# Attention units' exponentials, divisions, roundings and rests first on their engines, and head norms' scaling freed from the next tile's sums

## The chip, the cores and the metric

The kernel runs on one core of a Trainium2 chip. The metric is device time in microseconds (us) from the start to the end of one execution; less is better. TensorE (PE) multiplies matrices, VectorE (DVE) and ScalarE (ACT) do elementwise work, GpSimd (POOL) does small elementwise work and issues accumulating loads, SyncE (SP) issues most loads.

## The reference

One layer of a hybrid decoder trunk over 16 meta tokens and 512 real tokens, model width 1024, all in float32:

```python
h = h + 0.5 * swiglu(rms_norm(h, ffn1_norm), ffn1_w_in, ffn1_w_out)      # D_FF = 2816
h = h + token_mixer(rms_norm(h, mix_norm), ...)
h = h + 0.5 * swiglu(rms_norm(h, ffn2_norm), ffn2_w_in, ffn2_w_out)
return h[:, 128:]                                                        # real tokens only

def token_mixer(h, ...):
    qa, ka, va, fa, qb, kb, vb, ga, gb = split(h @ w_in)
    qa, ka, qb, kb = rms_norm of each head (64 wide), with a gain
    log_f = log_sigmoid(fa + forget_bias)
    o_fox = softmax(qa ka^T / 8 + cumsum(log_f)_q - cumsum(log_f)_k, causal) va        # 8 heads
    o_swa = softmax over a window of 128 keys, 16 meta keys and a sink, with a bias by distance   # 8 query, 2 key heads
    return (sigmoid(ga) * (o_fox @ w_branch_fox) + sigmoid(gb) * (o_swa @ w_branch_swa)) @ w_out
```

## The kernel before

Each float32 operand of a matmul is carried as two parts: a rounded part (`hi`, L130, a cast on ScalarE) and the rest (`lo`, L136, a subtraction on VectorE). A product is then three matmuls, L301, L302 and L304 in `prod`: rounded by rounded, rounded by rest, rest by rounded. Weights arrive by DMA as raw pieces and are split the same way in `split_to` (tiles wh and wl), up to three pieces ahead of their use. Most of the FFNs' products, and the gates', take seven half-size products instead of eight, with sums of inputs formed on VectorE (tc, S).

The program has three stages. The first FFN takes about the first 370 us, the token mixer and its output the next 370, the second FFN the rest. In the mixer two kinds of work are woven step by step into one stream (`weave`, `main` and `fills`, from L1628):

- attention units: eight `fox_pair` units (two query blocks of two heads each) and eight `swa_unit` units (one query block of four heads). A unit has `scores` (matmuls at L1292 for fox pairs, `prod` for sliding units; then VectorE adds the bias and takes the row minimum, L1310 or L1460; then `normalise`: exponentials on ScalarE with their sums, a reciprocal and a multiplication by it on VectorE, the "division"), `turn` (TensorE transposes, L1350 or L1473; a rounding into pH, a rest into pL or, for the meta keys, into other rows of pH), and `values` (matmuls at L1359 to L1365 or L1488 and L1490, then `both_halves` moves the result out of PSUM with ScalarE, L1105, and VectorE, L1106). A unit's `turn` and `values` stand behind the next unit's `scores`.
- fills: projections of queries, keys and values in chunks of up to five token tiles (`tok_chunk`), gates and branch products. A query or key tile goes through `head_norm`: squares on ScalarE (L1057), sums and a scaled shift on VectorE (L1058, L1059, the instruction kept in `shared["ts"]`), an inverse root on GpSimd (`rsq`, L351), and later the scaling (`scale`, L1073) on VectorE, which reads the projection out of PSUM and writes qn. `tok_chunk` traces the scaling of tile i - 1 behind the sums of tile i; the last tile's comes in the chunk's `end`. When all tiles are scaled, `finish` transposes qn (L1153, L1161, L1407) into the chunk's queries or keys.

Every engine runs its instructions in one fixed order, which a planner writes down ahead of the run: it goes through the program with a model of the time and, when an engine is free, takes among the instructions that are ready the one traced first. `tc.high_priority()` around instructions lets them be taken ahead of those traced before. `tc.issue_after(i)` and the kernel's `after(...)` place what is traced inside them, on the engine of instruction i, behind i in that engine's order; they wait for nothing else. PSUM tiles come in two groups of four banks, ps and pt, which the planner hands out again when the last reader is done.

In the mixer's end (L1646 to L1700) three gates go through sigmoids on ScalarE, held behind the last exponential by `after(shared["exp"])`, and are multiplied into the branch results on VectorE (L1654). Then the buffers of the mixer are given up, and the buffers of the gates' stage take their place, among them `spare` (L1695) and `xg`.

Of the kernel before, what the change touches and what calls it, by code (L numbers as in the profile page):

```python
# [13 lines left out]
AF = mybir.ActivationFunctionType  # L14
ALU = mybir.AluOpType
# [67 lines left out]
def kernel(  # L83
# [22 lines left out]
    V, A, G, PE, SP = nc.vector, nc.scalar, nc.gpsimd, nc.tensor, nc.sync  # L106
# [23 lines left out]
    def hi(o, i, scale=None):  # L130

        if scale is None:
            return A.copy(o, i)  # L133
        return A.activation(o, i, AF.Identity, scale=scale)

    def lo(o, i, h, scale=None):  # L136

        h = h.bitcast(F32)
        if scale is None:
            return V.tensor_tensor(out=o, in0=i, in1=h, op=ALU.subtract)  # L140
        else:
            return V.scalar_tensor_tensor(out=o, in0=i, scalar=scale, in1=h, op0=ALU.mult, op1=ALU.subtract)  # L142
# [59 lines left out]
    shared = {}  # L202
# [61 lines left out]
    def split_to(n):  # L264
        while state["split"] < min(n, len(pieces)):
            c = state["split"]
            load_to(c + 1)
            state["split"] += 1
            raw = raws.pop(c)
            if callable(raw):  # L270
                with tc.issue_after(shared["lo"]):
                    raw = raw()
            raw, nk, w = raw
            if pieces[c][0] == "D":
                wd = shared["wd"]()
                wh, wl = wd[:, :512], wd[:, 512:1024]
            else:
                wh, wl = (wp.tile([P, PW], F32R, tag=t, name=nm(t)) for t in ("wh", "wl"))
            b = slice(0, nk * w)
            shared["split"] = hi(wh[:, b], raw[:, b]), lo(wl[:, b], raw[:, b], wh[:, b])  # L280
            shared["lo"] = getattr(shared["split"][1], "ins", shared["split"][1])
            split[c] = tuple(t[:, : nk * w].rearrange("p (k c) -> p k c", c=w) for t in (wh, wl))

# [768 lines left out]
    def head_norm(ps, i, nh, outs):  # L1052

        n = M if i == 0 else P
        sq = new("hsq", [P, 256], F32, 3)
        ss = mp.tile([P, 4], F32, tag="hss", name=nm("hss"), bufs=4)[:n, :nh]
        A.activation(sq[:n, : nh * HD], ps[:n, : nh * HD], AF.Square)  # L1057
        V.tensor_reduce(out=ss, in_=sq[:n, : nh * HD].rearrange("p (h d) -> p h d", d=HD), axis=AX.X, op=ALU.add)  # L1058
        ts = V.tensor_scalar(ss, ss, r1sq[:n, i : i + 1], EPS, op0=ALU.mult, op1=ALU.add)  # L1059
        shared["ts"] = getattr(ts, "ins", ts)  # L1060
        rsq(ss, ss)
        src, by = ps[:n, : nh * HD].rearrange("p (h d) -> p h d", d=HD), bc(ss, 2, HD)

        def scale():

            with tc.issue_after(shared["ts"]):
                r = r1[:n, i : i + 1]
                for o in outs:
                    a, b = src, by
                    if isinstance(o, tuple):  # L1070
                        o, par = o
                        a, b = (v.rearrange("p (a b) d -> p a b d", b=2)[:, :, par] for v in (src, by))
                    V.scalar_tensor_tensor(out=o, in0=a, scalar=r, in1=b, op0=ALU.mult, op1=ALU.mult)  # L1073

        return scale
# [4 lines left out]
    def meta_rest(p, ps, w):  # L1080

        lo(p[REST : REST + M, :w], ps[:M, :w], p[:M, :w])
# [122 lines left out]
    def normalise(parts):  # L1205

        l = new("l", [P, 4], F32, 2)[:, : len(parts)]
        for j, (t, nmx) in enumerate(parts):
            shared["exp"] = A.activation(t, t, AF.Exp, bias=nmx, scale=-1.0, accum_out=l[:, j : j + 1])  # L1209
        V.reciprocal(l, l)  # L1210
        for j, (t, _) in enumerate(parts):
            V.tensor_scalar(t, t, l[:, j : j + 1], None, op0=ALU.mult)


    cbs = {}
# [33 lines left out]
    def fox_pair(box, p, ip, before):  # L1249
# [82 lines left out]
        def turn(hh):  # L1332
            if hh == 0:
                ps, pM = psum(), new("pH", [P, 512], bufs=3)
                for b in range(2):
                    c = column(0, 0, b)
                    PE.transpose(ps[:, P * b : P * b + P], ts_[b][:, c : c + P], ident)
                w = slice(0, 2 * P)
                hi(pM[:, w], ps[:, w])
                lo(pM[2 * REST :, w], ps[: 2 * REST, w], pM[: 2 * REST, w])  # L1340
                pts[0] = pM
            for j0 in range(1, nt, 2):
                ps = psum()
                pH, pL = new("pH", [P, 512], bufs=3), new("pL", [P, 512], bufs=3)
                c = 0
                for j in (j0, j0 + 1):
                    pts[j] = pH, pL, c - (P if j == nt - 1 else 0)
                    for b in range(1 if j == nt - 1 else 0, 2):
                        k0 = column(hh, j, b)
                        PE.transpose(ps[:, c : c + P], ts_[b][:, k0 : k0 + P], ident)  # L1350
                        c += P
                hi(pH[:, :c], ps[:, :c])
                lo(pL[:, :c], ps[:, :c], pH[:, :c])

        def values(hh):
            v = box["v"]
# [74 lines left out]
    def swa_unit(box, qbox, g, i, before):  # L1431
        nk = KS if i == 0 else KS + P
        k0 = 0 if i == 0 else KS * (i - 1)
        w = max(nk + nk % 2, 256)
        ts_, pts = [], []
        o = oA[:, 1, 2 * g : 2 * g + 2]

        tiles = [(0, 0), (1, M + 1)] if i == 0 else [(i, 0), (0, P), (i + 1, KS)]

        def scores():  # L1440
            before()
            q, k, b1 = qbox["q"], box["k"], b1s[g]
            room = new("t", [P, 1092], F32)
            for hp in range(2):
                t2 = room[:, 546 * hp : 546 * hp + 546]
                for hh in (2 * hp, 2 * hp + 1):
                    h = 4 * g + hh
                    hb = slice(64 * (hh % 2), 64 * (hh % 2) + 64)
                    ps = psum()
                    sq = (hb, hp, slice(P * i, P * i + P))  # L1450
                    sk = (hb, g, slice(k0, k0 + w))
                    prod([(ps[:, :w], k[0][sk], k[1][sk])], q[0][sq], q[1][sq], True, True)
                    t = t2[:, 273 * (hh % 2) : 273 * (hh % 2) + nk]
                    nmx = new("nmx", [P, 2], F32, 8)
                    init = 3.0e38
                    bias = (
                        [(M + 1, 0, P, b1[:, hh, KS:]), (0, P, KS, bm0[:, h])] if i == 0 else [(0, 0, nk, b1[:, hh])]
                    )
                    for pi, (to, a, b, bt) in enumerate(bias):
                        V.tensor_tensor_reduce(  # L1460
                            out=t[:, to : to + b - a], in0=ps[:, a:b], in1=bt, scale=-0.125, scalar=init,
                            op0=ALU.add, op1=ALU.min, accum_out=nmx[:, pi : pi + 1],
                        )
                        init = nmx[:, pi : pi + 1]
                    ts_.append((t, init))
            normalise(ts_)
            ts_[:] = [t for t, _ in ts_]

        def turn():
            for tt, c0 in tiles:  # L1470
                ps = psum()
                for hh in range(4):
                    PE.transpose(ps[:, P * hh : P * hh + P], ts_[hh][:, c0 : c0 + P], ident)  # L1473
                pH, pL = new("pH", [P, 512], bufs=3), None
                hi(pH, ps)
                if tt:
                    pL = new("pL", [P, 512], bufs=3)
                    lo(pL, ps, pH)
                else:
                    meta_rest(pH, ps, 512)  # L1480
                pts.append((pH, pL))

        def values():
            v = box["v"]
            pv = psum()
            for j, ((tt, c0), (pH, pL)) in enumerate(zip(tiles, pts)):
                st = v[:, tt, P * g : P * g + P]
                PE.matmul(pv, st, pH, start=j == 0, stop=False)  # L1488
                if tt:
                    PE.matmul(pv, st, pL, start=False, stop=j == len(tiles) - 1)  # L1490
            pvv = pv.rearrange("p (a b q) -> p a b q", b=2, q=P)
            for par in range(2):
                hb = slice(64 * par, 64 * par + 64)
                both_halves(o[hb, :, P * i : P * i + P], hb, pvv[:, :, par])

        return [scores, turn, values]
# [219 lines left out]

    def swa_out(m):
        return oA[:, m // 4, m % 4]

    def sliding(*ms):  # L1720
        for m in ms:
# [301 lines left out]
```

## Time and profile before

| | us |
|---|---|
| median of three runs (lowest, highest) | 1076.38 (1075.28, 1077.02) |
| the profiled execution, its own time | 1075.56 |
| its span, first to last instruction | 1073.5 |
| TensorE matmuls busy, share of the span | 1063.2 (99%) |
| VectorE busy | 892.0 (83%) |
| ScalarE busy | 654.6 (61%) |
| GpSimd busy | 211.7 (20%) |

Matmuls overlap in the array and their ends are modelled, so TensorE's busy share hides small holes; the waits of its weight loads (PEld) show them better. In a timeline row the columns are the start in us, the length in us, engine, line, operation, the tile written and those read, the shape and the count; a bracket gives the engine's idle time before it in us and what ended it. "issue" there means that the profile names no release. The granted clock of TensorE was 0.999.

### The profile page before, as it was taken

The page shows a single profiled execution, that of the slowest core. Times are in us where ns is not written, and L with a number is a line of the kernel's source. Part 1 is how long each engine was busy: PE and PEld are TensorE (multiplying, and loading weights), DVE is VectorE, ACT ScalarE, POOL GpSimd, SP SyncE. Part 2 cuts the span into 40 slices and gives each one's busy share as a digit, 9 for nine tenths or more (in the row PEclk, how much of TensorE's full clock was granted, in tenths as well). Part 3 has the DMA queues.
Part 4 walks back from the last instruction along what each step waited for, and adds up shares of the span by engine and source line. Part 5 has one row for each costly group of instructions (what it writes and reads, how often), then busy time and mean ns, then how long its engine had stood idle before and what let it go on. Part 6 is the DMA issues. An engine that isn't in the chain of part 4 may idle for free.

```text
span 1073.5 us, 22262 instructions
## 1 busy us (share of the span) xinstructions
PE 1063.2 (99%) x8515; PEld 1031.0 (96%) x8515; DVE 892.0 (83%) x1725; ACT 654.6 (61%) x1235; POOL 211.7 (20%) x281
## 2 busy tenths in 40 slices
PE   9999999999999999999999999999999999999998
PEld 8999999999999999999878799999999999999998
DVE  7988878888889678789897799888989788877895
ACT  7667456656666455556667766555665466745664
POOL 3011111121124442232200110001122111221120
PEclk9999999999999999999999999999999999999999
DMA  8787777688776314212211874567689777887763
GB/s 279 203 217 164 187 193 198 151 216 219 175 182 178 123 61 126 75 60 73 89 60 42 241 183 125 184 207 195 170 198 194 179 190 170 187 192 196 158 125 101
DMA packets 112570, 173.57 MB, mean 162 GB/s; under 512 B 10880, under 2 KB 59264, under 8 KB 112208
## 3 DMA queue, kind: packets, MB, share of 16 engines
q1 hardware_dynamic: 74464, 122.72, 36.2%
q0 software_dynamic: 29040, 37.83, 22.6%
q10 hardware_dynamic: 8960, 11.60, 3.4%
q8 instruction: 66, 1.08, 0.4%
q14 instruction: 40, 0.33, 0.1%
HBM read 167.89 MB, written 6.32 MB: 162 GB/s over the span
## 4 chain that ended last, share of the span: by engine, by line
PE 47%; DVE 5%; ACT 2%; DMA 1%; issue 1%; POOL 0%; ACTq 0%; SPq 0%; DVEq 0%; POOLq 0%
PE ps L301 8%; PE ps L304 8%; PE ps L302 8%; PE pt L301 7%; PE pt L302 7%; PE pt L304 7%; DVE wl L140 1%; DMA raw<-in_wg_dram 1%; ACT t L1209 1%; ACT wh L133 1%; DVE pL L140 1%; PE ps L1473 0%; PE ps L1938 0%; DVE S L140 0%; PE pt L1473 0%
## 5 line engine op out<-in xcount | busy, mean ns | idle before, releaser
L301 PE MATMUL ps<-x,wh 128*128 128x256 f32 (+2 forms) x768 | 219.7, 286 | 0.1
L302 PE MATMUL ps<-x,wh 128*128 128x256 f32 (+2 forms) x768 | 218.9, 285 | 0.5 <-DVE x L142 0.4
L304 PE MATMUL ps<-x,wl 128*128 128x256 f32 (+2 forms) x768 | 218.9, 285 | 0.0
L140 DVE TENSOR_TENSOR wl<-raw,wh 128x1024 fp32r<-128x1024 f32 (+3 forms) x125 | 150.1, 1201 | 39.8 <-ACT wh L133 38.9
L133 ACT CAST wh<-raw 128x1024 fp32r<-128x1024 f32 (+3 forms) x125 | 128.4, 1029 | 87.7 <-PE ps L302 52.5
L301 PEld LDWEIGHTS ps<-x,wh 128*128 128x128 f32 x768 | 144.7, 189 | 1.7 <-ACT hT L686 0.3
L302 PEld LDWEIGHTS ps<-x,wh 128*128 128x128 f32 x768 | 144.5, 188 | 1.4 <-DVE x L142 0.9
L304 PEld LDWEIGHTS ps<-x,wl 128*128 128x128 f32 x768 | 144.6, 188 | 0.9
L301 PE MATMUL pt<-x,wh 128*128 128x256 f32 (+2 forms) x424 | 125.3, 296 | 0.5 <-ACT wh L133 0.5
L304 PE MATMUL pt<-x,wl 128*128 128x256 f32 (+2 forms) x424 | 124.6, 294 | 0.0
L302 PE MATMUL pt<-x,wh 128*128 128x256 f32 (+2 forms) x392 | 112.5, 287 | 0.0
L133 ACT CAST wh<-tc 128x1024 fp32r<-128x1024 f32 (+1 forms) x70 | 71.8, 1026 | 65.1 <-DVE tc L234 55.7
L140 DVE TENSOR_TENSOR wl<-tc,wh 128x1024 fp32r<-128x1024 f32 (+1 forms) x70 | 83.5, 1192 | 32.4 <-ACT wh L133 32.0
L301 PE MATMUL ps<-acts,wh 128*128 128x264 f32 (+1 forms) x352 | 100.5, 285 | 0.1
L304 PE MATMUL ps<-acts,wl 128*128 128x264 f32 (+1 forms) x352 | 99.8, 284 | 0.0
L302 PE MATMUL ps<-acts,wh 128*128 128x264 f32 (+1 forms) x352 | 99.6, 283 | 0.0
L140 DVE TENSOR_TENSOR wl<-rawC,wh 128x1024 fp32r<-128x1024 f32 (+1 forms) x70 | 84.1, 1201 | 5.9 <-ACT wh L133 5.5
L133 ACT CAST wh<-rawC 128x1024 fp32r<-128x1024 f32 (+1 forms) x70 | 71.6, 1023 | 22.7 <-PE pt L302 17.7
L301 PEld LDWEIGHTS pt<-x,wh 128*128 128x128 f32 x424 | 79.9, 189 | 2.8 <-ACT wh L133 0.7
L304 PEld LDWEIGHTS pt<-x,wl 128*128 128x128 f32 x424 | 79.7, 188 | 2.1
L302 PEld LDWEIGHTS pt<-x,wh 128*128 128x128 f32 x392 | 73.8, 188 | 0.6
L301 PEld LDWEIGHTS ps<-acts,wh 128*128 128x128 f32 x352 | 66.5, 189 | 0.7 <-DVE h2T L918 0.3
(445 smaller groups left out, 3238.8 us busy)
## 6 DMA issues: line engine op xcount, KB each, us to landing
rawC<-in_w1i_dram SPq DMA_DIRECT2D x20, 512.0 KB, 5.1
raw<-in_w1i_dram SPq DMA_DIRECT2D x40, 256.0 KB, 4.5
raw<-in_w2i_dram SPq DMA_DIRECT2D x40, 256.0 KB, 3.3
rawC<-in_w2i_dram SPq DMA_DIRECT2D x20, 512.0 KB, 4.3
raw<-in_wm_dram SPq DMA_DIRECT2D x18, 512.0 KB, 4.3
raw<-in_wout_dram SPq DMA_DIRECT2D x16, 512.0 KB, 4.3
rawD<-in_w1i_dram SPq DMA_DIRECT2D x20, 256.0 KB, 4.3
raw<-in_w1i_dram POOLq DMA_DIRECT2D x20, 256.0 KB, 4.9
```

The source lines that it names most:

```text
L133: return A.copy(o, i)
L140: return V.tensor_tensor(out=o, in0=i, in1=h, op=ALU.subtract)
L301: PE.matmul(ps, sH, mH, start=first, stop=False, **more)
L302: PE.matmul(ps, sH, mL, start=False, stop=False, **more)
L304: shared["mm"] = PE.matmul(ps, sL, mH, start=False, stop=last, **more)
L1209: shared["exp"] = A.activation(t, t, AF.Exp, bias=nmx, scale=-1.0, accum_out=l[:, j : j + 1])
```

## The change

Five edits, all in the mixer:

- `normalise`: exponentials, reciprocal and divisions get high priority.
- `turn` of `fox_pair` and of `swa_unit`: the rounding and the rest of the transposed tile get high priority, and the rest is remembered in `shared["rests"]`. The rest of the very first tile of a fox unit (the meta keys, traced in `turn(0)`) is left as it was, and so are the meta keys' rests of the sliding units in the remembering.
- `split_to`: the rest of a weight piece is placed behind the unit rest remembered last, on VectorE.
- `head_norm`: the scaling is no longer placed behind the sums traced last.
- Before the sliding branch's products, the remembered rest is dropped.

```diff
@@ split_to
-            shared["split"] = hi(wh[:, b], raw[:, b]), lo(wl[:, b], raw[:, b], wh[:, b])
+            with after(*shared.get("rests", ())):
+                shared["split"] = hi(wh[:, b], raw[:, b]), lo(wl[:, b], raw[:, b], wh[:, b])
@@ head_norm
         def scale():
-            with tc.issue_after(shared["ts"]):
+            with ExitStack():
                 r = r1[:n, i : i + 1]
...
@@ normalise
-        for j, (t, nmx) in enumerate(parts):
-            shared["exp"] = A.activation(t, t, AF.Exp, bias=nmx, scale=-1.0, accum_out=l[:, j : j + 1])
-        V.reciprocal(l, l)
-        for j, (t, _) in enumerate(parts):
-            V.tensor_scalar(t, t, l[:, j : j + 1], None, op0=ALU.mult)
+        with tc.high_priority():
+            for j, (t, nmx) in enumerate(parts):
+                shared["exp"] = A.activation(t, t, AF.Exp, bias=nmx, scale=-1.0, accum_out=l[:, j : j + 1])
+            V.reciprocal(l, l)
+            for j, (t, _) in enumerate(parts):
+                V.tensor_scalar(t, t, l[:, j : j + 1], None, op0=ALU.mult)
@@ fox_pair, turn
-                hi(pH[:, :c], ps[:, :c])
-                lo(pL[:, :c], ps[:, :c], pH[:, :c])
+                with tc.high_priority():
+                    hi(pH[:, :c], ps[:, :c])
+                    shared["rests"] = [lo(pL[:, :c], ps[:, :c], pH[:, :c])]
@@ swa_unit, turn
-                hi(pH, ps)
                 if tt:
                     pL = new("pL", [P, 512], bufs=3)
-                    lo(pL, ps, pH)
-                else:
-                    meta_rest(pH, ps, 512)
+                with tc.high_priority():
+                    hi(pH, ps)
+                    if tt:
+                        shared["rests"] = [lo(pL, ps, pH)]
+                    else:
+                        meta_rest(pH, ps, 512)
@@ ahead of sliding
+    shared.pop("rests", None)
     def sliding(*ms):
```

## The prediction

> **What bounds the kernel now.** I read the page's engine totals first, then the busy time by stretches, then TensorE's waits in the mixer, then the chain of waits at the mixer's end, and last the order of instructions around single waits.
>
> ```profile
> span 1073.5 us, 22262 instructions
> PE 1063.2 (99%) x8515; PEld 1031.0 (96%) x8515; DVE 892.0 (83%) x1725; ACT 654.6 (61%) x1235; POOL 211.7 (20%) x281
> ```
>
> ```profile
> 440.00:600.00 160.00, 157.55 (x1114) 137.60 (x1114) 135.28 (x396) 103.65 (x257) 26.48 (x51) 1.00 0.23 72
> 700.00:800.00 100.00, 99.97 (x837) 99.17 (x836) 89.77 (x144) 61.36 (x101) 14.48 (x16) 1.00 0.70 188
> 470.00:490.00 20.00, 19.27 (x165) 17.94 (x162) 18.36 (x66) 13.13 (x37) 5.91 (x15) 1.00 0.16 41
> ```
>
> TensorE bounds the program: in the second FFN its matmuls fill 99.97 of 100 us and its weight loads 99.17. Nothing there is touched by the change, and nothing there can be won. The attention units lie between about 410 and 595 us. There TensorE's weight loads have holes, and VectorE (DVE) has 18.36 of 20 us of work at its densest. So the question is how much TensorE waits in that stretch, and for whom. The stretches' columns are the length, the busy time of TensorE (PE), of its weight loads, of VectorE, ScalarE and GpSimd, the granted clock and the DMA share. The first rows below are the weight-load queue's waits from 382 to 600 us (total, times, longest), the last one is a wait of the matmuls.
>
> ```profile
> PEld pt L1365 <- DVE pL L140: 2.2, 5, 0.7
> PEld pt L1488 <- ACT pH L133: 0.9, 1, 0.9
> PEld pt L1490 <- DVE pL L140: 0.8, 2, 0.6
> PEld pt L1350 <- DVE t L1212: 0.6, 2, 0.3
> PEld ps L1153 <- DVE qn L1073: 0.5, 2, 0.3
> ```
>
> ```profile
> PE ps L1473 <- DVE t L1212: 0.3, 1, 0.3
> ```
>
> That is the whole prize: waits for rests (pL), for roundings (pH), for divided tiles (t) and for head norms' scaling (qn). Added up it is under 6 us, 0.5% of the program, so no reading of this change gives more. The bound of what this kernel can tell from no change is about 0.2%, 2.15 us.
>
> **The rests (lo of pL) first on VectorE: 1.7 us won.** The five waits of L1365 are these rows of the weight-load queue, the wait in brackets.
>
> ```profile
> 463.38 0.19 PEld L1365 LDWEIGHTS pt<-pL,v 128*128 128x128 f32 x1 [0.23 <-DVE pL L140]
> 477.43 0.19 PEld L1365 LDWEIGHTS pt<-pL,v 128*128 128x128 f32 x1 [0.54 <-DVE pL L140]
> 489.61 0.19 PEld L1365 LDWEIGHTS pt<-pL,v 128*128 128x128 f32 x1 [0.31 <-DVE pL L140]
> 513.37 0.19 PEld L1365 LDWEIGHTS pt<-pL,v 128*128 128x128 f32 x1 [0.71 <-DVE pL L140]
> 525.35 0.19 PEld L1365 LDWEIGHTS pt<-pL,v 128*128 128x128 f32 x1 [0.37 <-DVE pL L140]
> ```
>
> They are of two kinds. Here is VectorE ahead of the wait at 489.61, and ScalarE's (ACT) rounding that its rest needs.
>
> ```profile
> 487.38 0.59 ACT L133 CAST pH<-ps 128x512 fp32r<-128x512 f32 x1
> 487.98 0.33 DVE L142 SCALAR_TENSOR_TENSOR v<-ps,r,v 128x128 fp32r<-128x128 f32 x1
> 488.36 0.59 DVE L1073 SCALAR_TENSOR_TENSOR qn<-ps,r,hss 128x128 f32<-128x128 f32 x2
> 488.88 0.67 DVE L140 TENSOR_TENSOR pL<-ps,pH 128x512 fp32r<-128x512 f32 x1
> ```
>
> The rounding was done at 487.97, the rest began at 488.88: a value's rest and two scalings stood in front, all ready earlier in the program's order. A higher priority moves the rest past them by 0.9 us, more than the 0.31 lost. At 477.43 and 525.35 the same kind of instructions stand in front, so I count these three whole: 0.54 + 0.31 + 0.37 = 1.22. The other kind is 513.37:
>
> ```profile
> 510.17 1.04 ACT L133 CAST wh<-raw 128x1024 fp32r<-128x1024 f32 x1
> 511.24 0.59 ACT L133 CAST pH<-pt 128x512 fp32r<-128x512 f32 x1
> 511.51 1.20 DVE L140 TENSOR_TENSOR wl<-raw,wh 128x1024 fp32r<-128x1024 f32 x1
> 512.64 0.67 DVE L140 TENSOR_TENSOR pL<-pt,pH 128x512 fp32r<-128x512 f32 x1
> ```
>
> A weight piece's rounding (1.04) and rest (1.20) went first while the unit's own source was not there yet. Priority alone does not help, since it cannot pass what has begun. The edit in the weight split does help: it queues the split's rest behind the unit rest traced last, which here takes 1.1 us out of the way. But it binds only if the split is traced after the turn, and it leaves ScalarE's cast in front. I count these two waits half, (0.23 + 0.71) / 2 = 0.47. Together 1.7, with ends 0 and 2.2.
>
> What that delays: a weight's rest waits for up to three unit rests of 0.67. Weights are split three pieces ahead of use, so I cost it at nothing; if that cover were gone, each late rest would cost up to 1.2, and the raw buffer's next load on SP's queue would start that much later (the DMA share is 0.23 in this stretch, so a transfer is not pressed). Below nothing it cannot be. No DMA is moved by the change.
>
> **Head norms' scaling freed: 1.2 us won, 0.6 lost.** VectorE and GpSimd (POOL) around a wait of scores for a bank:
>
> ```profile
> 431.55 1.98 POOL L351 TENSOR_TENSOR hss<-hss,nhalf 16x4 f32<-16x4 f32 x2
> 432.58 0.47 DVE L1073 SCALAR_TENSOR_TENSOR qn<-hsq,r,hss 16x256 f32<-16x256 f32 x1 [0.49 <-POOL hss L351]
> 434.78 0.42 DVE L1058 TENSOR_REDUCE hss<-hsq 128x4 f32<-128x256 f32 x1 [0.69 <-ACT hsq L1057]
> 435.24 0.23 DVE L1059 TENSOR_SCALAR hss<-hss,r1sq 128x4 f32<-128x4 f32 x1
> 435.38 0.60 DVE L1073 SCALAR_TENSOR_TENSOR qn<-ps,r,hss 128x128 f32<-128x128 f32 x2
> ```
>
> ```profile
> 436.10 0.18 PEld L1292 LDWEIGHTS ps<-kH,qH 64*128 64x128 f32 x1 [0.73 <-issue]
> 480.34 0.20 PEld L1350 LDWEIGHTS pt<-ident,t 128*128 128x128 f32 x2 [0.43 <-issue]
> ```
>
> The inverse roots ended at 433.53, yet the scaling, which frees the projection's PSUM bank, stood until the next tile's sums at 435.24 were through; VectorE idled 0.69 in between. Scores then waited 0.73. Freed, the scaling can run at about 434.1, behind the two rests there. A second bank wait, 0.43 before transposes, is alike. I take 0.73 + 0.43 = 1.2. The upper end adds the 0.5 of L1153, where a chunk's last scaling feeds the transposes directly.
>
> The loss: nothing now keeps a scaling from being queued directly behind its own sums, where VectorE then stands until GpSimd's inverse root is done. The first row counts the scalings' waits today (us, times), the second tells how long a root takes (min/median/max ns):
>
> ```profile
>   POOL hss L351: 1.8, 3
> ```
>
> ```profile
> L351 POOL TENSOR_TENSOR hss<-hss,nhalf x31: 687/1007/2305, 385.0 to 528.7; 128x4 f32<-128x4 f32 x24, 128x2 f32<-128x2 f32 x4, 16x4 f32<-16x4 f32 x2, 16x2 f32<-16x2 f32 x1
> ```
>
> Of the 31 head norms, the last of each of the seven chunks is free of a later tile's sums of its chunk already; 24 become free. Their price lies between 0 (other work stands between, as before most scalings now) and 0.6 each on VectorE (1.8 / 3). VectorE has 24.7 us of idle time between 440 and 600 (160 - 135.28), so most of this would be absorbed. I take 0.6 us on TensorE in all, one such wait unabsorbed; the ends are 0 and 7.2, which is 24 x 0.6 with half of it absorbed.
>
> **Exponentials and divisions first: 0.3 us won.** ScalarE's exponentials mostly wait for VectorE, not for a turn:
>
> ```profile
> ACT t L1209 <- DVE nmx L1460: 9.4, 7, 2.2
> ```
>
> And VectorE between two heads' divisions:
>
> ```profile
> 416.49 0.47 DVE L142 SCALAR_TENSOR_TENSOR v<-pt,r,v 128x256 fp32r<-128x256 f32 x1
> ```
>
> The scores' subtraction and minimum, which they wait for, gets no priority, so the exponentials themselves win nothing. A division does: the value's rest at 416.49 stands between the first head's division and the second's, and 0.47 of it goes, against one of the two 0.3 waits of L1350. I take 0.3, the ends are 0 and 0.9 (L1350 and L1473). The scores' subtractions get later: up to three unit rests (3 x 0.67) may now pass them. I cost that at nothing because a unit's turn comes only after other units' and projections' matmuls; if that cover is gone it is the 0.3 of L1473 that grows.
>
> **The mixer's end: nothing counted.** L1488 and L1490 wait at 591 to 592 us, 0.9 and 0.8, behind sigmoids. But the chain of waits runs there without TensorE:
>
> ```profile
> 580.64 0.45 PE pt L1473 x4
> 581.13 0.58 ACT pH L133
> ...
> 600.01 7.83 DMA raw<-in_wg_dram
> ...
> 622.02 0.39 PE pt L301
> ```
>
> From 581.13 to 622.02 it is ScalarE, VectorE and one load. A wait removed at 591 returns before 622.02 unless that chain is shorter, and the sigmoids' products (L1654) have to be done before the buffers behind it are free, whatever their order. So nothing, with 1.7 us as the better end. What TensorE wins before 580 does count, since its transposes at 580.64 start this chain.
>
> **The sum.** 1.7 + 1.2 + 0.3 - 0.6 = 2.6 us. The profiled execution took 1075.56 us (span 1073.5 and 2.1 around it); it lies 0.8 below the median of the runs, 1076.38. 1075.56 - 2.6 = 1073.0.
>
> **Rival one: the order hardly changes where TensorE waits (no measurable change).** For it: two of five rest waits have an instruction in front that began before the unit's was ready, VectorE's work stays the same, and at 470 to 490 us it is 92% full, so what moves forward pushes a projection's evacuation back by as much. Against it: 477 to 525 shows ready rests passed over. Then only the scalings' 1.2 is won against 0.6 lost: 1075.0.
>
> **Rival two: VectorE stands for GpSimd (slower).** Place: every freed scaling, in front of whose root nothing else is queued; the high priority cannot pass it, for it is at the queue's head. Without the loss I have 3.2 us won, so the measured slowdown (above 1078.5) needs 6.1 us on TensorE, 0.26 for each of 24 scalings. At half of the 0.6 seen, 7.2 us, the time is 1075.56 - 3.2 + 7.2 = 1079.6. For it: the 0.49 at 432.58 and the mean of 0.6, though scalings are held back now. Against it: VectorE's backlog at 470 to 490 leaves little empty queue, and only three scalings waited at all. A longer root would make it worse:
>
> ```profile
> 511.28 2.31 POOL L351 TENSOR_TENSOR hss<-hss,nhalf 128x4 f32<-128x4 f32 x1 [2.31 <-DVE hss L1059]
> ```
>
> It ran beside the weight's rest of 511.51 and took 2.31, where the median root takes 1.01. The Trainium skill, "SBUF — State Buffer", section "Who interferes with whom", says that a VectorE instruction with two SBUF inputs contends with a GpSimd one that reads SBUF, and that the loser blocks for the whole instruction. By that rule the 1.3 us at 511 is such a block, and a freed scaling behind it would hold VectorE 1.3 longer: the sum would come to 1074.3 with one such meeting and to 1075.6 with two. By the rows, one root in 31 is that long (the median is 1007 ns), and the sum stays.
>
> **Chances.** Forecast 0.46, rival one 0.39, rival two 0.15. Below 1074.2 is faster: 0.46; up to 1078.5 the same: 0.39; slower: 0.15. The better ends of all terms together (2.2 + 1.7 + 0.9 + 1.7, no loss) give 1069.1, all at once unlikely; without the mixer's end it is 1070.8. The range goes from 1070.8 to 1077.6, short of rival two; the forecast's own is 1071.5 to 1074.2.
>
> **What would show it.** Right: L1365's wait for pL falls from 2.2 to about 0.5; no "issue" wait of 0.73 before scores at 436; scalings stand in front of the next tile's sums; weight rests follow unit rests. Wrong: the row of L1073's wait for POOL grows from 1.8 towards 7 and more (rival two); or L1365's wait stays near 2 (rival one); or the waits at 621 to 622 grow by what was won before 580.

## The result, and the profile after

The changed kernel takes 1093.27 us (median of five runs, 1092.71 to 1096.84) against 1076.72 for the kernel before. The ratio of the two kernels' runs, 1.0165 with a 95% interval of 1.0153 to 1.0177, is formed from the single runs and is not the quotient of the two medians (1.0154). By the medians it is 16.5 us slower, and the forecast was 1073.0. The profiled execution, whose rows follow, took 1096.84 us with a span of 1093.7; it is the longest of the five, 3.6 us above their median. The changed kernel's lines lie a few further on: L351 is L352 there, L1073 is L1074, L1365 is L1368, L1695 is L1700.

The page's totals, then busy time by stretches (length, TensorE, weight loads, VectorE, ScalarE, GpSimd, granted clock, DMA share, GB/s):

```profile
span 1093.7 us, 22272 instructions
PE 1069.1 (98%) x8515; PEld 1036.8 (95%) x8515; DVE 894.4 (82%) x1725; ACT 655.0 (60%) x1235; POOL 213.7 (20%) x281
```

```profile
382.00:410.00 28.00, 22.64 (x189) 21.90 (x188) 17.39 (x49) 12.46 (x23) 10.87 (x17) 1.00 0.21 65
410.00:600.00 190.00, 178.13 (x1308) 160.80 (x1309) 148.44 (x443) 106.71 (x271) 36.69 (x73) 0.96 0.22 69
800.00:900.00 100.00, 100.00 (x844) 100.00 (x843) 82.86 (x136) 58.27 (x99) 20.77 (x20) 1.00 0.84 190
```

The same stretch at the start in the kernel before:

```profile
382.00:410.00 28.00, 27.81 (x233) 27.08 (x233) 21.40 (x56) 14.86 (x27) 11.72 (x20) 1.00 0.30 97
```

No work was added: the engines' busy times and counts are those of before within 6 us. In the 28 us from 382 on, 189 matmuls start instead of 233, though no attention unit is at work yet, only projections with their head norms. VectorE is less busy too, 17.39 us for 21.40, so TensorE does not wait for an engine that is full. The second FFN is as full as before. The mixer's end dates the loss: this row is VectorE's first work behind it, first in the kernel before, then in the changed one.

```profile
595.98 2.50 DVE L1695 TENSOR_TENSOR spare<-x 128x512 f32<-128x512 f32 x4
```

```profile
616.10 2.50 DVE L1700 TENSOR_TENSOR spare<-x 128x512 f32<-128x512 f32 x4
```

It comes 20.1 us later, which is the whole difference of the two spans (1093.7 - 1073.5 = 20.2). Now VectorE's waits from 382 to 600 us (total, times, longest), and TensorE's:

```profile
DVE qn L1074 <- POOL hss L352: 27.6, 25, 2.8
DVE hss L1059 <- ACT hsq L1058: 4.1, 6, 1.3
```

```profile
PE ps L303 <- DVE wl L140: 2.9, 1, 2.9
PE pt L1007 <- DVE wl L140: 2.7, 1, 2.7
PE pt L1368 <- DVE pL L140: 2.4, 2, 2.1
PE ps L1368 <- DVE pL L140: 2.0, 2, 1.9
PE ps L1294 <- DVE qn L1074: 1.8, 2, 1.2
PE ps L1294 <- DVE qH L142: 1.3, 1, 1.3
PE ps L1476 <- DVE t L1214: 1.2, 1, 1.2
```

The scalings' wait for the inverse root was 1.8 us in 3 places and is 27.6 in 25. TensorE's seven rows above add up to 14.3 us; the longest such row in the kernel before was this one:

```profile
PE pt L1365 <- DVE pL L140: 1.0, 3, 0.5
```

TensorE now waits for whatever stood behind a scaling in VectorE's queue: weights' rests (wl), unit rests (pL), queries. One such place, VectorE first, then GpSimd, then TensorE:

```profile
455.17 0.23 DVE L1060 TENSOR_SCALAR hss<-hss,r1sq 128x4 f32<-128x4 f32 x1
456.59 0.35 DVE L1074 SCALAR_TENSOR_TENSOR qn<-pt,r,hss 128x128 f32<-128x128 f32 x1 [1.19 <-POOL hss L352]
456.86 0.55 DVE L140 TENSOR_TENSOR pL<-ps,pH 128x384 fp32r<-128x384 f32 x1
```

```profile
455.54 1.01 POOL L352 TENSOR_TENSOR hss<-hss,nhalf 128x4 f32<-128x4 f32 x1 [2.41 <-DVE hss L1060]
```

```profile
457.46 0.39 PE L1368 MATMUL ps<-pL,v 128*128 128x256 f32 x1 [1.87 <-DVE pL L140]
```

The scaling stands directly behind its own shift, VectorE idles 1.19 us for the root, and a unit rest of high priority waits behind it. TensorE loses 1.87. Priority decides who is queued first, not who may pass once VectorE has stopped.

### The profile page after: what moved, and what is told of

The parts are those of the page before. It is cut to its first block, busy times and chain, and to the rows that moved or that the text cites. A ratio compares the mean times of both kernels' runs of the same rounds, so it can differ in the third digit from the quotient of the medians.

```text
span 1093.7 us, 22272 instructions
## 1 busy us (share of the span) xinstructions
PE 1069.1 (98%) x8515; PEld 1036.8 (95%) x8515; DVE 894.4 (82%) x1725; ACT 655.0 (60%) x1235; POOL 213.7 (20%) x281
## 4 chain that ended last, share of the span: by engine, by line
PE 46%; DVE 3%; ACT 2%; DMA 1%; issue 1%; POOL 0%; ACTq 0%; DVEq 0%; POOLq 0%
PE ps L302 8%; PE ps L303 8%; PE ps L305 8%; PE pt L302 7%; PE pt L303 7%; PE pt L305 7%; DMA xg<-h1d 1%; PE ps L1476 1%; DVE wl L140 0%; ACT wh L133 0%; ACT xg L1735 0%; POOL hss L352 0%; PE ps L1945 0%; ACT t L1211 0%; PE pt L1476 0%
```

## The experiments

**The change without the freed scaling, and the freed scaling alone.** Theory A says that VectorE's standing for GpSimd is the loss; theory B that the priorities cost by themselves.

```diff
 # e1: the changed kernel
-            with ExitStack():
+            with tc.issue_after(shared["ts"]):
                 r = r1[:n, i : i + 1]
 # e2: the kernel before
-            with tc.issue_after(shared["ts"]):
+            with ExitStack():
                 r = r1[:n, i : i + 1]
```

> All edits of the change but one: the scaling stands again behind the next tile's sums. Theory A (VectorE stands for GpSimd's roots at the freed scalings; nothing else costs much): VectorE's wait of the scalings for the root falls from 27.6 us to about 2, no half-speed spell of TensorE's clock, and the time is 1072 to 1077. Theory B (the priorities and the queued weight rests push projections' and weights' work back and cost several us by themselves): the root waits fall too, but the time stays at 1080 or more.

> The kernel before with the one edit that frees the scaling; no priorities, no queued weight rests. Theory A: the scalings' waits for roots are 20 to 28 us, and the time is 1088 to 1096. Theory B: the time is at most 1084, since the rest of the loss needs the priorities.

With the scaling queued again: 1076.32 us, ratio 1.0003 (0.9994 to 1.0012). With the scaling freed and nothing else: 1090.61 us, ratio 1.0137 (1.0121 to 1.0154). VectorE's wait in the one and in the other:

```profile
DVE qn L1074 <- POOL hss L352: 2.3, 4, 1.0
```

```profile
DVE qn L1073 <- POOL hss L351: 25.9, 25, 2.4
```

So theory A holds, and the one line makes nearly all of the loss. The step from 1.0137 to 1.0165 is hardly outside the two intervals (1.0154 and 1.0153 are their near ends); if it is real, it belongs to the other edits in the freed order. The changed kernel has one wait of TensorE for a unit rest (1.9 us) that the kernel with the freed scaling alone does not have. Which edit brings that was not tried.

**Priorities alone.**

```diff
 # the change with the scaling queued, and
-            with after(*shared.get("rests", ())):
+            with ExitStack():
                 shared["split"] = hi(wh[:, b], raw[:, b]), lo(wl[:, b], raw[:, b], wh[:, b])
```

> The kernel before with the high priorities alone; the scaling is queued as before and weight rests are not tied to unit rests. Theory A: 1073 to 1078, the wait of the values' matmuls for pL under 2.2 us. Theory B: above 1080. Against the first kernel of this call it tells what tying the weight rests is worth: I expect under 1 us either way.

1075.75 us, ratio 1.0001 (0.9992 to 1.0010). The priorities are worth nothing, with or without the tie. But they did what they say: in the kernel with the scaling queued, the weight loads' wait for rests fell from 2.2 to 1.4 us, and another took its place.

```profile
PEld pt L1368 <- DVE pL L140: 1.4, 4, 0.7
PEld ps L1476 <- issue: 1.4, 1, 1.4
```

VectorE, and the weight load that came late, in that kernel:

```profile
530.93 0.69 DVE L140 TENSOR_TENSOR pL<-pt,pH 128x512 fp32r<-128x512 f32 x1
531.54 1.22 DVE L140 TENSOR_TENSOR wl<-raw,wh 128x1024 fp32r<-128x1024 f32 x1
532.67 0.44 DVE L1463 CUSTOM_DVE_ANT_0 t<-pt,cb 128x273 f32<-128x273 f32 x1
535.53 1.18 DVE L1214 TENSOR_SCALAR t<-t,l 128x273 f32<-128x273 f32 x4
536.01 0.89 PEld L1476 LDWEIGHTS ps<-ident,t 128*128 128x128 f32 x4 [1.45 <-issue]
```

The weight's rest, now behind the unit rest, stands in front of the next unit's scores, and their exponentials and divisions come as much later: the divisions start at 535.53 here and at 534.77 in the kernel before.

**The freed scaling without its wait.** The scaling reads the shifted sums, so it never waits for GpSimd, first in the freed and then in the queued place. These two kernels leave the inverse root out of their result; GpSimd still forms it.

```diff
 # the changed kernel (the second: with the scaling queued)
-        rsq(ss, ss)
+        root = mp.tile([P, 4], F32, tag="hsr", name=nm("hsr"), bufs=4)[:n, :nh]
+        rsq(root, ss)
```

> The changed kernel in full, but the scaling reads the shifted sums instead of their inverse roots; GpSimd still forms the roots, into another tile that nobody reads. So the scalings are free and never wait for GpSimd. Theory A: the root waits are gone, and the time is 1070 to 1077. Theory B: it stays at 1080 or more. A third reading, that freed scalings are bad because they stand in VectorE's queue ahead of other work rather than because they wait: also 1080 or more, without root waits.

> As the kernel that scales with the shifted sums in place of their roots (GpSimd's roots go unread), but with the scaling queued behind the next tile's sums. It tells what part of that kernel's 0.2% came from the scaling's earlier place and what from the root's own length at the chunks' ends. If the earlier place is worth what I priced (1.2 us for two bank waits and up to 0.5 at the chunks' ends): 1075 to 1077, 1 to 3 us above it. If the root's length was what counted: 1073 to 1074, the same as it.

Freed: 1073.35 us, ratio 0.9980 (0.9970 to 0.9989). Queued: 1075.51 us, ratio 1.0001 (0.9992 to 1.0010). So the earlier place is good by itself, about 2 us, and a root of the length that it has costs nothing behind the next tile's sums. All of the loss is the wait, none of it the order.

**Dose.** Freed for odd tiles only, and freed in the sliding keys' chunk only:

```diff
 # the kernel before
-            with tc.issue_after(shared["ts"]):
+            with ExitStack() if i % 2 else tc.issue_after(shared["ts"]):     # half freed
+            with ExitStack() if nh == 2 else tc.issue_after(shared["ts"]):   # keys' chunk freed
```

> The kernel before with the scaling freed for odd token tiles only, 14 of the 24 scalings that the change frees. Theory A (the loss is VectorE standing for each freed scaling's root): the scalings' wait for roots is about 14/24 of the 25.9 us of the kernel with all of them freed, 13 to 16 us, and the time lies between, 1080 to 1087. Rival (the loss comes from two or three unlucky places, such as the late weight rests at 394 and 410 us): the time is near one of the ends, under 1079 or above 1088.

> The kernel before with the scaling freed only in the sliding keys' chunk (its four scalings that a later tile's sums held). In the changed kernel these had hardly any root wait, since VectorE had other work queued there. Theory A: no more than 2 us of root waits, the bank wait of 0.4 us at 480 us gone, time 1073 to 1077, perhaps 0.1% better than before. Rival (freeing a scaling is harmful wherever it stands): 1078 or more.

Half freed: 1079.15 us, ratio 1.0034 (1.0021 to 1.0048). Keys' chunk: 1074.84 us, ratio 0.9996 (0.9987 to 1.0005), so the gain I hoped for is not measurable. The first row is the half freed kernel's, the second that of the keys' chunk:

```profile
DVE qn L1073 <- POOL hss L351: 10.1, 16, 1.2
```

```profile
DVE qn L1073 <- POOL hss L351: 2.1, 4, 1.0
```

Where VectorE has other work queued, as in the keys' chunk, a freed scaling hardly waits: one of this chunk's five did, 0.48 us, and the other three places are those of the kernel before. The half dose misses my numbers: 8.3 us of added waits cost 3.9 us (1079.15 against 1075.28), the full 24.1 cost 15.1 (1090.61 against 1075.49). By waits that is 0.47 and 0.63 per us. That more standing is covered less well is one reading of it; another is TensorE's clock, which fell to half in four stretches of the fully freed kernel and in none of the half freed one's mixer (see below). These runs do not part the two.

**A longer root, queued.**

```diff
 # the kernel before
+        for _ in range(3):
+            G.tensor_copy(ss, ss)
         rsq(ss, ss)
```

> The kernel before, scaling queued as it was, but GpSimd does three small copies in the place ahead of each root, so each root comes some 0.6 us or more later. Theory A: behind the next tile's sums the root is covered for several us, so the time is within 2 us of the kernel before. Rival (the root's length is on the path in any order, and the chunks' ends show it): 1080 or more.

1080.02 us, ratio 1.0043 (1.0030 to 1.0057): just the rival's number. The copies' row, and VectorE's wait:

```profile
L1062 POOL COPY hss<-hss 128x4 f32<-128x4 f32 (+3 forms) x93 | 21.9, 235 | 40.1 <-DVE hss L1059 36.4
```

```profile
DVE qn L1075 <- POOL hss L351: 6.3, 8, 1.7
```

Each root came 0.7 us later (3 x 0.235), and 4.5 us of added waits cost 4.7, about one for one. But the chunks' ends, which the rival named, are not where the scalings wait. All eight waits lie between 389 and 438 us, and seven of them directly behind the next tile's sums; only the one at 411.09 (0.85 us) is a chunk's last scaling. So the cover behind the next tile's sums is just long enough for the root as it is in the first chunks, and ample only later, where attention work stands between: behind 438 us no scaling waits.

**The clock.** The changed kernel's granted clock was 0.96 from 410 to 600 us. It ran at half speed in four stretches of 3.41 us, each behind a stretch in which TensorE had stood for 1.1 us or more; so did the kernel with the scaling freed alone. Two of the latter's, each with the stretch ahead of it:

```profile
390.20:393.60 3.40, 1.11 (x10) 0.90 (x8) 2.24 (x7) 0.93 (x1) 1.01 (x1) 1.00 0.01 2
393.60:397.00 3.40, 2.80 (x13) 2.80 (x14) 2.46 (x5) 0.04 (x1) 1.85 (x1) 0.50 0.46 140
407.30:410.70 3.40, 1.40 (x12) 1.19 (x12) 2.18 (x5) 1.32 (x2) 1.07 (x2) 1.00 0.64 195
410.70:414.10 3.40, 3.40 (x19) 3.40 (x18) 2.06 (x4) 0.55 (x2) 3.01 (x5) 0.50 0.86 320
```

At most that is 4 x 3.41 x 0.5 = 6.8 us. To tell whether it is a part of the loss, the kernel with the scaling freed alone got idle matmuls in the two longest waits, and the kernel before the same as a control:

```diff
+            if half and i == tiles[0]:
+                shared["chunk"] = shared.get("chunk", 0) + 1
+                if shared["chunk"] in (2, 3):
+                    spare_bank = psum()
+                    for _ in range(6):
+                        PE.matmul(spare_bank, xH[:, 0, :P], xH[:, 1, :512], start=True, stop=True)
             for k in range(4 * half, 4 * half + 4):
                 tok_step(box[i], i, w, k, 256)
```

> The kernel with the freed scaling alone (ratio 1.0137 to the kernel before, four half-speed stretches of TensorE's clock), plus six idle matmuls of 512 columns (about 0.23 us each) into an unread bank, at the two places where TensorE waited 2.9 and 2.0 us for a weight's rest. They fit into those waits and keep the array active there. Theory C (part of the loss is the clock: after a stretch of 3.4 us with little array activity the next 3.4 us run at half speed, some 1.7 us each): the half-speed stretches at 393.6 and 410.7 us go, two are left, the time falls by 2 to 3.5 us, ratio 1.0105 to 1.0125. Rival (the half speed only shows where TensorE waits anyway and costs nothing): the time stays within 1 us or rises, ratio 1.013 to 1.016, whether the stretches go or not.

> The same twelve idle matmuls in the kernel before, where TensorE does not wait at those places: their own cost, 12 x 0.23 = 2.7 us if all of it counts, so 1076.5 to 1079; half of that if small waits near by absorb some.

Filled: 1091.58 us, ratio 1.0146 (1.0129 to 1.0163). The control: 1080.01 us, ratio 1.0031 (1.0018 to 1.0044). The two stretches went; these are the filled kernel's rows in their place.

```profile
392.90:396.40 3.50, 1.97 (x15) 1.65 (x15) 3.39 (x6) 0.02 (x1) 0.98 (x2) 1.00 0.12 40
396.40:399.80 3.40, 3.11 (x28) 2.82 (x27) 1.28 (x6) 1.45 (x3) 1.91 (x2) 1.00 0.67 228
```

```profile
394.77 0.39 PE L302 MATMUL ps<-wl,x 128*128 128x256 f32 x1 [1.53 <-DVE wl L140]
```

The wait there fell from 2.9 to 1.53, by the idle matmuls' time, so they cost nothing at that place, and half speed was avoided twice. Yet the time did not fall. The traces tell more than the time does. Here are the mixer's first projection, the second of the two waits and VectorE's first work behind the mixer, first with the scaling freed alone, then filled:

```profile
376.33 0.36 PE L1005 MATMUL pt<-wh,xm 128*128 128x256 f32 x1
410.22 0.39 PE L1006 MATMUL pt<-wl,xm 128*128 128x256 f32 x1 [2.00 <-DVE wl L140]
611.60 2.50 DVE L1695 TENSOR_TENSOR spare<-x 128x512 f32<-128x512 f32 x4
```

```profile
376.89 0.36 PE L1005 MATMUL pt<-wh,xm 128*128 128x256 f32 x1
410.72 0.39 PE L1006 MATMUL ps<-wl,xm 128*128 128x256 f32 x1 [1.31 <-DVE wl L140]
610.83 2.50 DVE L1701 TENSOR_TENSOR spare<-x 128x512 f32<-128x512 f32 x4
```

From the first row to the second it is 33.89 us and 33.83: the first half-speed stretch cost nothing, since TensorE waited for VectorE behind it anyway, as the rival says. From the first to the third it is 235.27 and 233.94: without the second stretch the mixer was 1.3 us shorter in these two executions, of at most 1.7. The whole time hides this, because both filled kernels lose it again at the program's end, where ScalarE waits for an output's store; TensorE's wait there is 0.5 us in the kernel before and with the scaling freed alone, and in the filled kernel it is this (1.9 us in the control, whose mixer the twelve idle matmuls made 2.2 us longer):

```profile
PE ps L1944 <- ACT out L1945: 1.7, 1, 1.7
```

So neither theory holds whole. The clock is a part of the loss, but a consequence of the waits; the other two stretches were not filled, and what they cost is open.

**A try at a better version.**

```diff
 # the kernel before, sliding keys' chunk freed, and
-        V.tensor_reduce(out=ss, ...)
+        red = V.tensor_reduce(out=ss, ...)
-        shared["ts"] = getattr(ts, "ins", ts)
+        shared["ts"] = getattr(red, "ins", red)
```

> A try at a better version: the kernel before with the scaling queued behind the next tile's first sum instead of the shift behind it (0.23 us earlier, the root done long before), and free in the sliding keys' chunk. Theory A: root waits at most 3 us, time 1073 to 1076, equal to the kernel before or up to 0.2% better. Rival (even a little earlier is harmful): 1078 or more.

1077.76 us, ratio 1.0018 (1.0009 to 1.0026), slightly slower, with the scalings waiting 6.1 us for roots in 8 places. No kernel here that computes the whole reference beats the kernel before measurably.

## Why the prediction was wrong

The step that failed is the freed scaling's loss, "I take 0.6 us on TensorE in all". The runs showed that this one line costs 15.1 us alone (1090.61 against 1075.49), with 24.1 us of added waits on VectorE. The place was rival two's, and so was the mechanism; size and chance (0.15) were not, and even rival two's 1079.6 was 14 us short.

- *Price.* I took 0.6 us for each from the three waits of the kernel before. All three scalings stood behind the next tile's sums, and in two of them GpSimd had begun the root late, behind its other work (copies ahead of 402.80, a mask ahead of 432.58). They say nothing of a scaling directly behind its own shift, which waits for a whole root, and the row for that stood in the prediction, median 1007 ns. The 25 waits of the changed kernel are 1.1 us each on average (27.6 / 25).
- *Number.* I let only some of 24 land behind their own shift. Of the 25 that waited, 17 stand directly behind it and make 22.0 of the 27.6 us; the other eight have one instruction between. Nor was 24 the number of freed scalings: five of the seven chunks trace their last scaling only after the next chunk's first sums (`LAG`, L1546 and L1629 to L1631), so that the line held these too, and 29 of the 31 became free. In the kernel before, the first chunk's last scaling (394.07) stands behind a shift of the next chunk (393.93).
- *Cover.* I set the waits against VectorE's 24.7 us of idle time. That idle time is not free: 21.5 us of it are waits of VectorE, 18.7 for ScalarE and 2.8 for TensorE; its longest two rows from 440 to 600 us are below. A wait at the queue's head stops everything behind it. Of 25.8 us added on VectorE, 20 arrived in the profiled execution's span, and 16.5 by the medians.

```profile
DVE l L1210 <- ACT t L1209: 3.8, 4, 1.1
DVE hss L1058 <- ACT hsq L1057: 3.1, 5, 1.1
```

The other terms. *Bank waits, 1.2 won*: about right, the freed order without its wait gave some 2 us, and the scores' waits for a bank (0.9 us with the scaling queued) are gone from its trace. *Rests, 1.7 won*: 0.8 of it came, and it went back into a wait that I had named as the one to grow, the 0.3 of L1473, now 1.2 on the matmul and 1.4 on its weight load. *Exponentials, 0 to 0.3*: nothing seen. So without the freed scaling, rival one would have held (1076.32 and 1075.75), and its reason, that what moves forward pushes something else back by as much, is what the rows show. *The mixer's end, 0*: nothing was seen against it.

The rule that I weighed fits better than I judged. The Trainium skill, "SBUF — State Buffer", section "Who interferes with whom", says that of a VectorE instruction with two SBUF inputs and a GpSimd one that reads SBUF, the one issued second blocks. In the changed kernel:

```profile
528.07 1.23 DVE L140 TENSOR_TENSOR wl<-raw,wh 128x1024 fp32r<-128x1024 f32 x1
530.20 0.48 DVE L1074 SCALAR_TENSOR_TENSOR qn<-ps,r,hss 128x256 f32<-128x256 f32 x1 [0.90 <-POOL hss L352]
```

```profile
528.10 2.06 POOL L352 TENSOR_TENSOR hss<-hss,nhalf 128x4 f32<-128x4 f32 x1 [2.31 <-DVE hss L1060]
```

The root that started just behind a weight's rest took 2.06 us instead of 1.01, and one at 395.24, 0.23 us behind the start of another rest, took 1.85. That agrees. In the kernel before, though, the root of 511.28 took 2.31 us and had started 0.23 us ahead of the rest, so by these starts it was not always the second that lost. Such a meeting makes single waits: both scalings here waited 0.90 us, where the rest would have covered an ordinary root. It isn't the cause: these are 1.8 of 27.6 us, and all but three of the 31 roots took no more than 1.01 us; the third took 1.29.

## What to carry to other kernels

An ordering line that looks like a mere delay may be the only thing that keeps an engine from stopping at its queue's head; price its removal by the full latency of what the freed instruction waits for, times all the places, before any gain. Idle time on the engine is a poor cover for such a stop when others are queued behind it: 24.1 us of added waits cost 15.1 here. And a higher priority among instructions that share a nearly full engine moves waits about; count what it pushes back as carefully as what it pulls forward.

## What the hardware showed

TensorE's clock fell to half for 3.41 us after stretches of the same length with a wait of TensorE in them. The Trainium skill, "TensorE: Matmul & The Clock Gate", section "Part 1: The HAM clock gate", describes such a free-running window of 3.41 us with the half rate behind an idle one. Here the stretches were not idle: ten matmuls started in the first, twelve in the second, with waits of 2.9 and 2.0 us. The number of starts alone does not tell which stretch is followed by half speed: one with 21 (481.6 to 485.0 us of the changed kernel) was, one with 14 (392.9 to 396.3 us, clock 1.00 in the one behind it) was not. These runs show no rule for it. Unexpected too was that half speed cost nothing in the one place where TensorE then waited for VectorE anyway, and some 1.3 us in the other.
